# A decoder trunk on one NeuronCore: DeltaNet decays from two shared operands, conv taps and gathers on GpSimd, solve steps placed behind the weight splits

## The chip, the cores and the metric

The kernel runs on one core of one Trainium2 chip. A core has a matrix engine (PE; PEld is its weight loading, which overlaps), a vector engine (DVE), a scalar engine (ACT), a general engine (GpSimd, POOL in the profile) and a queue processor (SP) that issues the DMAs. The engines run side by side; each takes its own instructions strictly in their order, and an instruction waits at the head of its engine until the semaphores it names have been reached. The metric is device time of one execution in microseconds (us), lower is better. "Before" is the median of 3 runs, and the profile is of a further execution.

## The reference

Two layers over 512 positions of 1024 channels. Layer 0 mixes tokens with a gated DeltaNet, layer 1 with a Conformer convolution; each is followed by cross-attention into a memory of 256 rows and a squared-ReLU MLP. Only the DeltaNet is touched. Cut to what matters (8 heads of width 128; chunks of 64 in the reference, of 128 in the kernel):

```python
proj = h @ w_in                                    # q, k, v, z and 16 gate columns
qkv  = silu(causal_depthwise_conv(qkv, w_conv))    # width 4
beta = sigmoid(b_raw)
g    = -exp(a_log) * softplus(a_raw + dt_bias)     # log decay per token and head
g_cum = cumsum(g, axis=-1)                         # inside a chunk
diff  = g_cum[..., :, None] - g_cum[..., None, :]
decay = exp(where(causal, diff, -inf))
lower = where(strict, (k_beta @ k.T) * decay, 0)
sol   = triangular_solve(I + lower, [v*beta, k_beta*exp(g_cum)])
attn_intra = (q @ k.T) * decay
# then the scan over chunks: v_new, o, state
```

## The kernel before

**The stream of units.** All large products run as units. A unit is 24 matmuls of 128x128 weights by 512 columns that fill one PSUM bank: 8 input tiles, each as three products of split numbers (`mm3`: high by high, high by low, low by high). The weights of a unit (128x1024) come by DMA as `raw`; ACT rounds them to `wh` (`wsplit`, L204) and DVE computes the rest `wl` = raw - wh (L205, printed as L72, the line of the helper `tt`). Three such pairs exist (NW = 3), so the pair of a unit can be made only when the unit three places earlier has left PE.

**The DeltaNet stage** covers about the first 330 us. Its units run in the order k0 to k7, v0 to v3, q0 to q3, z (heads 0 to 3), v4 to v7, q4 to q7, z, and then the keys and values of the first cross-attention. Each unit is cut into two halves ("mains"); `run` goes through the mains by number, and after main i it records the side jobs that `S.at(i, rank, ...)` hung there, by rank. k2 is mains 6 and 7, v0 18 and 19, q0 26 and 27, q3 32 and 33, z begins at 34. A scheduler then fixes each engine's order of instructions once, at build time; nothing is reordered on the chip.

**The side jobs of one k head**, which the change touches:

- `gates` (after main 5): from the 16 gate columns `ab` come `beta` and `g`, by about 25 small DVE operations on 128x32 tiles and three ACT exponentials.
- `decay_in`: for each head GpSimd builds `gi` = tri_le times g (128x512), ACT and DVE split it into `gih` and `gil`. `decay`: PE multiplies both with `tri_gt_r` into PSUM, ACT takes the exponential (`dt`), GpSimd multiplies by the mask `tri_le` (L406).
- `conv_head`: DVE scales the unit's PSUM result into `cv`, ACT makes tap 0 (`cva`), and each further tap is either one DVE operation (L422) or an ACT product `cvq` (L419) and a GpSimd addition (L420); CONV_K, CONV_Q and CONV_V say how many taps go the second way. Then ACT applies SiLU.
- `k2`: PE transposes k (`kt`, L440) and forms its Gram matrix (`G`, L444); ACT squares and copies, DVE multiplies with the decay into `bt`, GpSimd scales `bt`.
- `fs_in` (L485): four ACT copies of 32x128 gather the diagonal 32x32 blocks of `bt` into `DB`, for all heads together.

**The solve.** `fs_begin` transposes DB into `FT` on DVE (L499), and `fs_steps` runs 31 steps of two dependent DVE operations each (`fst`, `X`, L508 and L510), with FS = (23, 9): from main 23 on, over 9 mains. `fs_end` transposes twice (`TB`, `UB`). `mg_a` copies the blocks back (ACT to `x0`, GpSimd to `u0`), and `mg_w` and `mg_y` merge them on PE (`mg`, L545 and L557) from main 32 on (MG). `q2` forms `ai` = k times q (L466), `rec` is the scan over the chunks from main 41 on (REC), and both need what stands above.

Of the kernel before, what the change touches and what calls it, by code (L numbers as in the profile page):

```python
# [8 lines left out]
F32 = mybir.dt.float32  # L9
F32R = mybir.dt.float32r  # L10
# [30 lines left out]
def tile_trunk(ctx, tc, xT, memT, prm_d, adt_d, bdw_d, w_ab, w_kq, w_v, w_z, w_dno, w_pw1, w_pw2,  # L41
# [5 lines left out]
    wp = ctx.enter_context(tc.tile_pool(name="wp", bufs=2))  # L47
    fsp = ctx.enter_context(tc.tile_pool(name="fsp", bufs=3))
    up = ctx.enter_context(tc.tile_pool(name="up", bufs=NSLOT))
    sp = ctx.enter_context(tc.tile_pool(name="sp", bufs=16))  # L50
    psp = ctx.enter_context(tc.tile_pool(name="psp", bufs=8, space=bass.MemoryType.PSUM))

    cnt = [0]
# [15 lines left out]
        return cp.tile(list(shape), dt, tag=s, name=s)  # L69

    def tt(e, o, a, b, op):
        e.tensor_tensor(out=o, in0=a, in1=b, op=op)  # L72

    def stt(o, a, s, b, op0, op1):
        dve.scalar_tensor_tensor(out=o, in0=a, scalar=s, in1=b, op0=op0, op1=op1)  # L75
# [43 lines left out]
    for i in range(WARM):  # L119
# [4 lines left out]
    tri_gt = const([P, P], "tri_gt")  # L124
    pool.affine_select(out=tri_gt, in_=ones, pattern=[[-1, P]], compare_op=ALU.is_gt, fill=0.0,
                       base=0, channel_multiplier=1)
    tri_gt_r = const([P, P], "tri_gt_r", F32R)
    act.copy(tri_gt_r, tri_gt)
    ident4 = const([P, 32], "ident4")
    eps_rms = const([P, 1], "eps_rms")  # L130
    pool.memset(eps_rms, EPS)
# [64 lines left out]
    def wsplit():  # L196
        u = ws["split"]
        ws["split"] += 1
        while ws["load"] <= u:
            wload()  # L200
        raw = ws["raw"].pop(u)
        h = wp.tile([P, 1024], F32R, tag="wh", name=nm("wh"), bufs=NW)
        lo = wp.tile([P, 1024], F32R, tag="wl", name=nm("wl"), bufs=NW)
        act.copy(h, raw)  # L204
        tt(dve, lo, raw, h.bitcast(F32), ALU.subtract)  # L205
        ws["hl"][u] = (h, lo)

    def wnext(key, hf):
# [118 lines left out]
    class DeltaNet:  # L327
        def __init__(self, norm):
            self.n, self.xs = norm, norm.xs
            for n, s in ((64, "abt"), (32, "beta"), (32, "g"), (96, "egd"), (32, "sek"), (32, "nk"),  # L330
                         (32, "s_all"), (32, "sdec"), (32, "s_neg"), (32, "sdec_neg"), (32, "ssq"), (4, "tok")):
                setattr(self, s, keepc(n, s))
            for s in ("GI", "DtM", "KT", "Kt", "Ai", "QT", "BT", "U", "VT", "VB", "Z", "OG", "ps", "M"):
                setattr(self, s, {})
            self.DB = self.fs = None
            self.S = [None, None]
# [46 lines left out]
            ts(dve, e2, e1, 1.0, ALU.add)  # L383
            dve.reciprocal(beta, e2)

        def decay_in(self, hs):
            for h in hs:
                gi = slot(s="gi")
                tt(pool, c4(gi), over_c(tri_le), over_i(self.g[:, h * 4:h * 4 + 4]), ALU.mult)
                self.GI[h] = split(gi, "gi")  # L390

        def decay(self, hs):
            if 0 in hs:
                ps_g = psum("gsum")
                pe.matmul(ps_g[:, 0:32], ones, self.g, start=True, stop=True)
                pe.matmul(ps_g[:, 32:64], tri_gt, self.g, start=True, stop=True)
                pe.matmul(ps_g[:, 64:96], tri_le, self.g, start=True, stop=True)
                act.activation(self.egd, ps_g[:, 0:96], AF.Exp)
            for h in hs:
                gh, gl = self.GI.pop(h)  # L400
                ps = psum("dt")
                pe.matmul(ps, tri_gt_r, gh, start=True, stop=False)
                pe.matmul(ps, tri_gt_r, gl, start=False, stop=True)
                dt = slot(s="dt")
                act.activation(dt, ps, AF.Exp)
                tt(pool, c4(dt), c4(dt), over_c(tri_le), ALU.mult)  # L406
                self.DtM[h] = dt

        def conv_head(self, ps, ti, npool, a=None):
# [19 lines left out]
            self.KT[h] = self.conv_head(self.ps.pop(("k", h)), 8 + h, CONV_K)  # L429

        def ev_q(self, h):
            self.M["q", h] = self.conv_head(self.ps.pop(("q", h)), h, CONV_Q)

        def k2(self, h):
            hc = slice(h * 4, h * 4 + 4)
            gq = h // 4
            kT = self.KT[h]
            ps = psum("kt")
            for c in range(4):
                pe.transpose(ps[:, c * P:(c + 1) * P], kT[:, c * P:(c + 1) * P], ident)  # L440
            psg = psum("G")
            for c in range(4):
                cs = slice(c * P, (c + 1) * P)
                pe.matmul(psg[:, cs], kT[:, cs], kT[:, cs], start=True, stop=True)  # L444
            sqk = slot(s="sqk")
            act.activation(sqk, ps, AF.Square)
            kt = slot(s="kt")
            act.copy(kt, ps)
            self.Kt[h] = kt
            bt0 = self.BT[h] = slot(s="bt")  # L450
            tt(dve, bt0, psg, self.DtM[h], ALU.mult)
            ssk = small(4)
            dve.tensor_reduce(out=ssk, in_=c4(sqk), op=ALU.add, axis=AX.X)
            ts(dve, self.sek[:, hc], ssk, EPS, ALU.add)
            rk = small(4)
            dve.reciprocal(rk, self.sek[:, hc])
            tt(dve, self.s_all[:, hc], rk, self.beta[:, hc], ALU.mult)
            tt(pool, c4(bt0), c4(bt0), over_i(self.s_all[:, hc]), ALU.mult)
# [26 lines left out]
        def fs_in(self, h):  # L485
            bt, n = c4(self.BT[h]), h * 4
            if self.DB is None:
                self.DB = fsp.tile([P, 1024], F32, tag="fs", name=nm("DB"))
            db = self.DB.rearrange("p (i n) -> p i n", n=32)
            for b in range(4):  # L490
                bs = slice(32 * b, 32 * b + 32)
                act.copy(db[bs, :, n:n + 4], bt[bs, :, bs].rearrange("p c i -> p i c"))

        def fs_begin(self):
            X = fsp.tile([P, 1024], F32, tag="fs", name=nm("X"))
# [659 lines left out]
    for gq in range(2):  # L1155
        S.at(at["z", "g", gq] + 7, 4, D.ev_z, gq)
    S.at(T_STAT + 3, 0, D.gates)
    S.at(T_STAT + 5, 5, D.decay_in, [0, 1, 2, 3])
    S.at(T_DEC, 2, D.decay, [0, 1])
    S.at(T_DEC + 1, 2, D.decay, [2, 3])  # L1160
    for i, hh in enumerate(([4, 5], [6, 7])):
        S.at(DEC1[i], 5, D.decay_in, hh)
        S.at(DEC1[i] + 2, 2, D.decay, hh)
    for h in range(8):
        S.at(K2[h], 2, D.k2, h)
        S.at(K2[h] + 2, 5, D.fs_in, h)
# [1 line left out]
        S.at(Q2[h] + 1, 3, D.q3, h)  # L1168
    f0, nf = FS
    S.at(f0, 5, D.fs_begin)  # L1170
    for i in range(nf):
        S.at(f0 + i, 6, D.fs_steps, i * 31 // nf, (i + 1) * 31 // nf)
    S.at(f0 + nf, 0, D.fs_end)
    for h in range(8):
        S.at(MGP[h], 5, D.mg_pre, h)
        S.at(MG[h], 1, D.mg_a, h)
        for j, f in enumerate((D.mg_w, D.mg_y, D.mg_y, D.mg_end)):
            S.at(MG[h] + MGLAG + j, 1, f, h)
    for gq in range(2):
        S.at(f0 + 1 + gq, 7, D.norm_k, gq)  # L1180
        for c in range(4):
            S.at(at["v", 4 * gq + 3] + V2[gq], 3, D.v2, gq, c)
        n = 0
        for c in range(4):
            for step in range(3):
                S.at(REC[gq] + n, 0, D.rec, gq, c, step)
                n += 1
            S.at(REC[gq] + n, 5, D.o_gate, gq, c)
        S.at(REC[gq] + n + 1, 1, D.o_norm, gq)
# [117 lines left out]
WARM = 13  # L1307
SQ0 = 8
T_STAT = 2
T_DEC = 10  # L1310
NW = 3
CONV_K, CONV_Q, CONV_V = 0, 1, 3
DEC1 = (11, 13)
K2 = (13, 12, 14, 15, 16, 17, 19, 20)
Q2 = (30, 31, 33, 35, 54, 56, 58, 60)
FS = (23, 9)
MGP = (31, 31, 34, 34, 37, 37, 40, 40)
MG = (32, 32, 35, 35, 38, 38, 41, 41)
MGLAG = 1
V2 = (8, 7)  # L1320
MGAIN = 4
HO = 73
REC = (41, 66)
MEM = 53
MLP_ORDER = [("up", 0), ("up", 1), ("dn", 0), ("up", 2), ("dn", 1), ("up", 3), ("dn", 2), ("dn", 3)]
TAP_RATE = 0.75
# [95 lines left out]
```

## Time and profile before

| | |
|---|---|
| median of 3 runs | 1596.11 us (1595.97 to 1596.54) |
| the profiled execution: its time, its span | 1595.83 us, 1594.1 us |
| mean granted PE clock | 0.985 |
| PE, DVE, ACT, POOL busy | 97%, 56%, 42%, 17% of the span |
| PE busy in the stretches 0-40, 40-80, 80-120, 120-160, 160-200 us | 36.01, 34.26, 36.26, 22.83, 37.30 us |
| PE busy from 200 to 240 and from 400 to 480 us | 40.00 and 80.00 us, that is all of it |

The page gives the busy time of each engine, then strips of 40 slices in tenths. The granted clock is the share of full speed that PE was given: at 1.00 the matmuls of a unit follow each other every 0.23 us, at half clock every 0.43 us. In the timeline, a row has its start in us, its length, engine, line, operation, the tile written, the tiles read, shapes and a count; in brackets the idle time of that engine ahead of it and who ended that. Rows of groups have the busy time and then the mean of one in ns.

### The profile page before, as it was taken

To read this page: it belongs to the slowest core of one execution; us is meant where nothing else is said; L and a number is where in the kernel's file an instruction comes from. 1 tells how busy PE (TensorE), PEld (TensorE's weight loads), DVE (VectorE), ACT (ScalarE), POOL (GpSimd) and SP (SyncE) were. 2 spreads that over 40 slices of the span, in tenths; PEclk is the share of its full clock that TensorE was granted. 3 is DMA by queue.
4 is the path that set the end of the run, shared out by engine and by line. 5 is a ranking of instruction groups with operands and counts; after the bars stand their busy time and mean duration, and the time that the engine had idled before them with its cause. 6 is when DMAs were issued, how large, how long until landed. Compare 5 with 4: busy or idle time off the path is not lost.

```text
span 1594.1 us, 19919 instructions
## 1 busy us (share of the span) xinstructions
PE 1543.3 (97%) x7864; PEld 1304.3 (82%) x7864; DVE 893.1 (56%) x1239; ACT 663.3 (42%) x1014; POOL 273.4 (17%) x310
## 2 busy tenths in 40 slices
PE   8895999999999999999999999899999999999997
PEld 6674888898888888888888889888888888888897
DVE  6969447576455444343445599974445443444443
ACT  6694546545344443241324321264434442323332
POOL 0653434302111100000021316102112000000002
PEclk9997999999999999999999999999999999999999
DMA  5112012254221232322322422252213223222321
GB/s 179 49 58 66 29 65 80 67 186 131 93 66 65 87 101 93 105 94 93 102 96 93 144 81 78 76 171 94 79 40 106 93 93 96 102 93 95 104 93 54
DMA packets 47615, 147.09 MB, mean 92 GB/s; under 512 B 6305, under 2 KB 11041, under 8 KB 47521
## 3 DMA queue, kind: packets, MB, share of 16 engines
q1 hardware_dynamic: 47520, 145.81, 27.6%
q8 instruction: 62, 1.02, 0.3%
q14 instruction: 33, 0.26, 0.0%
HBM read 142.38 MB, written 2.10 MB: 91 GB/s over the span
## 4 chain that ended last, share of the span: by engine, by line
PE 82%; DVE 11%; ACT 3%; issue 2%; POOL 1%; DMA 0%; DVEq 0%; SPq 0%; POOLq 0%; ACTq 0%
PE dn L220 7%; PE dn L222 7%; PE dn L221 7%; PE up L220 7%; PE up L222 7%; PE up L221 7%; DVE ca L75 4%; PE q L220 2%; PE xo L221 2%; PE q L222 2%; PE q L221 2%; PE xo L222 2%; PE xo L220 2%; DVE wl L72 2%; PE pw L220 2%
## 5 line engine op out<-in xcount | busy, mean ns | idle before, releaser
L204 ACT CAST wh<-raw 128x1024 fp32r<-128x1024 f32 x248 | 259.9, 1051 | 690.7 <-PE dn L221 191.5
L72 DVE TENSOR_TENSOR wl<-raw,wh 128x1024 fp32r<-128x1024 f32 x248 | 314.2, 1269 | 130.3 <-ACT wh L204 124.3
L220 PE MATMUL up<-xh,wh 128*128 128x512 f32 x512 | 200.2, 391 | 0.0
L222 PE MATMUL up<-xh,wl 128*128 128x512 f32 x512 | 199.2, 389 | 0.0
L221 PE MATMUL up<-xl,wh 128*128 128x512 f32 x512 | 199.2, 389 | 0.0
L220 PE MATMUL dn<-uh,wh 128*128 128x512 f32 x448 | 174.3, 389 | 0.0
L221 PE MATMUL dn<-ul,wh 128*128 128x512 f32 x448 | 174.3, 389 | 0.0
L222 PE MATMUL dn<-uh,wl 128*128 128x512 f32 x448 | 174.3, 389 | 0.0
L72 DVE TENSOR_TENSOR h<-dn,h 128x512 f32<-128x512 f32 x56 | 41.8, 747 | 170.4 <-PE dn L222 170.4
L75 DVE SCALAR_TENSOR_TENSOR rl<-up,rb 128x512 f32<-128x512 f32 x64 | 44.2, 690 | 157.0 <-PE up L222 157.0
L72 POOL TENSOR_TENSOR tap<-ident,prm 128x512 f32<-128x512 f32 x45 | 60.5, 1373 | 331.4 <-PE up L222 263.8
L221 PEld LDWEIGHTS up<-xl,wh 128*128 128x128 f32 x512 | 96.1, 188 | 20.3 <-issue 0.5
L220 PEld LDWEIGHTS up<-xh,wh 128*128 128x128 f32 x512 | 96.1, 188 | 20.3 <-issue 0.5
L222 PEld LDWEIGHTS up<-xh,wl 128*128 128x128 f32 x512 | 96.1, 188 | 20.1
L222 PEld LDWEIGHTS dn<-uh,wl 128*128 128x128 f32 x448 | 84.1, 188 | 17.5
L221 PEld LDWEIGHTS dn<-ul,wh 128*128 128x128 f32 x448 | 84.1, 188 | 17.4
L220 PEld LDWEIGHTS dn<-uh,wh 128*128 128x128 f32 x448 | 84.1, 188 | 17.4
L72 POOL TENSOR_TENSOR sq<-sq,sq 128x512 f32<-128x512 f32 x30 | 49.7, 1658 | 257.7 <-ACT sq L295 177.0
L220 PE MATMUL h<-xh,wh 128*128 128x512 f32 x192 | 81.2, 423 | 6.1 <-ACT wh L204 3.7
L75 DVE SCALAR_TENSOR_TENSOR ca<-x,prm,ca 128x512 f32<-128x512 f32 x90 | 81.8, 910 | 2.1
L222 PE MATMUL h<-xh,wl 128*128 128x512 f32 x192 | 78.0, 406 | 3.9 <-DVE wl L72 3.9
L221 PE MATMUL h<-xl,wh 128*128 128x512 f32 x192 | 77.8, 405 | 0.3 <-DVE xl L75 0.3
(326 smaller groups left out, 3162.4 us busy)
## 6 DMA issues: line engine op xcount, KB each, us to landing
raw<-w_up SPq DMA_DIRECT2D x64, 512.0 KB, 3.4
raw<-w_dn SPq DMA_DIRECT2D x64, 512.0 KB, 3.4
raw<-w_pw SPq DMA_DIRECT2D x24, 512.0 KB, 3.6
raw<-w_kq SPq DMA_DIRECT2D x16, 512.0 KB, 3.8
raw<-w_k SPq DMA_DIRECT2D x16, 512.0 KB, 3.9
raw<-w_vv SPq DMA_DIRECT2D x16, 512.0 KB, 3.6
raw<-w_q SPq DMA_DIRECT2D x16, 512.0 KB, 3.4
raw<-w_o SPq DMA_DIRECT2D x16, 512.0 KB, 3.6
```

Of the source, the lines that this page charges most:

```text
L72: e.tensor_tensor(out=o, in0=a, in1=b, op=op)
L75: dve.scalar_tensor_tensor(out=o, in0=a, scalar=s, in1=b, op0=op0, op1=op1)
L204: act.copy(h, raw)
L220: pe.matmul(ps, wh, xh, start=first, stop=False)
L221: pe.matmul(ps, wh, xl, start=False, stop=False)
L222: pe.matmul(ps, wl, xh, start=False, stop=last)
```

## The change

- **Decays.** `decay_in` now works for all heads at once. Two operands are made: `R` (128x512) and `L` (128x1024), whose constant halves `decay_const` fills early on GpSimd from two indicator tables `ind` and `headm` (three new DVE reductions beside the setup). When g is there, DVE spreads it to `grep` (128x128), one PE matmul with `tri_mid` makes the sums (`ct`), ACT and DVE split them (`V`), and DVE fills the other halves of R and L. For each head, `decay` adds two products in PSUM: the identity by the mask `later` (0 or -1e30) and a slice of L by R. The exponential of that is `dt`, with no mask after it. The GpSimd `gi`, the splits of `gi` and the GpSimd mask go. `decay_in` hangs at main 5 behind `gates`; the `ct` matmul stands in PE's built order ahead of unit k2.
- **Taps.** CONV_K goes from 0 to 2, CONV_Q from 1 to 3 for heads 0 to 3 (1 stays for 4 to 7).
- **Gathers.** `fs_in` copies with GpSimd in place of ACT.
- **Keys again.** The copy `kt` of heads 4 to 7 moves out of `k2` to `kt2` at mains 60 to 63, which transposes them a second time (16 PE transposes).
- **Solve.** `fs_steps` is recorded under `issue_after(ws["last"])`: in the built order each group of steps stands behind the newest `wl`. FS is (23, 12).
- **Places.** K2, Q2, MGP, MG, REC and the decays move, as the last lines show; the pool of small tiles goes from 16 to 13 buffers.

```diff
     up = ctx.enter_context(tc.tile_pool(name="up", bufs=NSLOT))
-    sp = ctx.enter_context(tc.tile_pool(name="sp", bufs=16))
+    sp = ctx.enter_context(tc.tile_pool(name="sp", bufs=13))
     psp = ctx.enter_context(tc.tile_pool(name="psp", bufs=8, space=bass.MemoryType.PSUM))
...
     def tt(e, o, a, b, op):
-        e.tensor_tensor(out=o, in0=a, in1=b, op=op)
+        return e.tensor_tensor(out=o, in0=a, in1=b, op=op)
     def stt(o, a, s, b, op0, op1):
...
                        base=0, channel_multiplier=1)
-    tri_gt_r = const([P, P], "tri_gt_r", F32R)
-    act.copy(tri_gt_r, tri_gt)
+    ident_r = const([P, P], "ident_r", F32R)
+    act.copy(ident_r, ident)
+    later = const([P, P], "later", F32R)
+    ts(pool, later, tri_le, 1.0, ALU.subtract, 1e30, ALU.mult)
+    tri_mid = const([P, P], "tri_mid")
+    ts(pool, tri_mid, tri_le, tri_le[:, 63:64], ALU.subtract)
+    ind = const([P, 4], "ind")
+    dve.tensor_reduce(out=ind, in_=ident.rearrange("p (x c) -> p c x", c=4), op=ALU.add, axis=AX.X)
+    headm = const([P, 8], "headm")
+    headx = const([P, 32], "headx")
+    dve.tensor_reduce(out=headx, in_=ident.rearrange("p (x c) -> p x c", c=4), op=ALU.add, axis=AX.X)
+    dve.tensor_reduce(out=headm, in_=headx.rearrange("p (a h) -> p h a", h=8), op=ALU.add, axis=AX.X)
     ident4 = const([P, 32], "ident4")
...
         act.copy(h, raw)
-        tt(dve, lo, raw, h.bitcast(F32), ALU.subtract)
+        ws["last"] = tt(dve, lo, raw, h.bitcast(F32), ALU.subtract).ins
         ws["hl"][u] = (h, lo)
...
             for n, s in ((64, "abt"), (32, "beta"), (32, "g"), (96, "egd"), (32, "sek"), (32, "nk"),
-                         (32, "s_all"), (32, "sdec"), (32, "s_neg"), (32, "sdec_neg"), (32, "ssq"), (4, "tok")):
+                         (32, "s_all"), (P, "grep"), (32, "sdec"), (32, "s_neg"), (32, "sdec_neg"), (32, "ssq"), (4, "tok")):
                 setattr(self, s, keepc(n, s))
...
             dve.reciprocal(beta, e2)
-        def decay_in(self, hs):
-            for h in hs:
-                gi = slot(s="gi")
-                tt(pool, c4(gi), over_c(tri_le), over_i(self.g[:, h * 4:h * 4 + 4]), ALU.mult)
-                self.GI[h] = split(gi, "gi")
+        def decay_const(self):
+            self.R = slot(F32R, "R")
+            self.L = fsp.tile([P, 1024], F32R, tag="fs", name=nm("L"))
+            pool.tensor_copy(c4(self.R)[64:128], over_i(ind)[64:128])
+            pool.tensor_copy(self.L.rearrange("p (h j) -> p h j", h=8)[0:64], over_i(headm)[0:64])
+        def decay_in(self):
+            dve.tensor_copy(self.grep.rearrange("p (a x) -> p a x", a=4), over_c(self.g))
+            ps = psum("ct")
+            pe.matmul(ps[:, 0:P], self.grep, tri_mid, start=True, stop=True)
+            v = slot(F32R, "V")[:, 0:P]
+            act.copy(v, ps[:, 0:P])
+            for a in (1, 3):
+                rs = slice(32 * a, 32 * a + 32)
+                tt(dve, v[rs], ps[rs, 0:P], v[rs].bitcast(F32), ALU.subtract)
+            vf = v.bitcast(F32)
+            tt(dve, c4(self.R)[0:64], over_c(vf)[0:64], over_i(ind)[0:64], ALU.mult)
+            stt(self.L.rearrange("p (h j) -> p h j", h=8)[64:128], over_c(vf, 8)[64:128], -1.0,
+                over_i(headm)[64:128], ALU.mult, ALU.mult)
         def decay(self, hs):
...
             for h in hs:
-                gh, gl = self.GI.pop(h)
                 ps = psum("dt")
-                pe.matmul(ps, tri_gt_r, gh, start=True, stop=False)
-                pe.matmul(ps, tri_gt_r, gl, start=False, stop=True)
+                pe.matmul(c4(ps), ident_r, over_c(later), start=True, stop=False)
+                pe.matmul(ps, self.L[:, h * P:(h + 1) * P], self.R, start=False, stop=True)
                 dt = slot(s="dt")
                 act.activation(dt, ps, AF.Exp)
-                tt(pool, c4(dt), c4(dt), over_c(tri_le), ALU.mult)
                 self.DtM[h] = dt
...
         def ev_q(self, h):
-            self.M["q", h] = self.conv_head(self.ps.pop(("q", h)), h, CONV_Q)
+            self.M["q", h] = self.conv_head(self.ps.pop(("q", h)), h, CONV_Q[h // 4])
+        def tr_k(self, h):
+            ps = psum("kt")
+            for c in range(4):
+                pe.transpose(ps[:, c * P:(c + 1) * P], self.KT[h][:, c * P:(c + 1) * P], ident)
+            return ps
+        def kt2(self, h):
+            ps = self.tr_k(h)
+            self.Kt[h] = slot(s="kt")
+            act.copy(self.Kt[h], ps)
         def k2(self, h):
...
             kT = self.KT[h]
-            ps = psum("kt")
-            for c in range(4):
-                pe.transpose(ps[:, c * P:(c + 1) * P], kT[:, c * P:(c + 1) * P], ident)
+            ps = self.tr_k(h)
             psg = psum("G")
...
             act.activation(sqk, ps, AF.Square)
-            kt = slot(s="kt")
-            act.copy(kt, ps)
-            self.Kt[h] = kt
+            if h < 4:
+                self.Kt[h] = slot(s="kt")
+                act.copy(self.Kt[h], ps)
             bt0 = self.BT[h] = slot(s="bt")
...
                 bs = slice(32 * b, 32 * b + 32)
-                act.copy(db[bs, :, n:n + 4], bt[bs, :, bs].rearrange("p c i -> p i c"))
+                pool.tensor_copy(db[bs, :, n:n + 4], bt[bs, :, bs].rearrange("p c i -> p i c"))
         def fs_begin(self):
...
     S.at(T_STAT + 3, 0, D.gates)
-    S.at(T_STAT + 5, 5, D.decay_in, [0, 1, 2, 3])
-    S.at(T_DEC, 2, D.decay, [0, 1])
-    S.at(T_DEC + 1, 2, D.decay, [2, 3])
-    for i, hh in enumerate(([4, 5], [6, 7])):
-        S.at(DEC1[i], 5, D.decay_in, hh)
-        S.at(DEC1[i] + 2, 2, D.decay, hh)
+    S.at(0, 4, D.decay_const)
+    S.at(T_STAT + 3, 1, D.decay_in)
+    for i in range(4):
+        S.at(T_DEC + i, 2, D.decay, [2 * i, 2 * i + 1])
     for h in range(8):
...
     S.at(f0, 5, D.fs_begin)
+    def fs_steps(j0, j1):
+        with tc.issue_after(ws["last"]):
+            D.fs_steps(j0, j1)
     for i in range(nf):
-        S.at(f0 + i, 6, D.fs_steps, i * 31 // nf, (i + 1) * 31 // nf)
+        S.at(f0 + i, 6, fs_steps, i * 31 // nf, (i + 1) * 31 // nf)
     S.at(f0 + nf, 0, D.fs_end)
...
             S.at(MG[h] + MGLAG + j, 1, f, h)
+    for h in range(4, 8):
+        S.at(KT2 + h, 2, D.kt2, h)
     for gq in range(2):
...
 T_STAT = 2
-T_DEC = 10
+T_DEC = 9
 NW = 3
-CONV_K, CONV_Q, CONV_V = 0, 1, 3
-DEC1 = (11, 13)
-K2 = (13, 12, 14, 15, 16, 17, 19, 20)
-Q2 = (30, 31, 33, 35, 54, 56, 58, 60)
-FS = (23, 9)
-MGP = (31, 31, 34, 34, 37, 37, 40, 40)
-MG = (32, 32, 35, 35, 38, 38, 41, 41)
+CONV_K, CONV_Q, CONV_V = 2, (3, 1), 3
+K2 = (11, 12, 13, 14, 15, 16, 18, 20)
+Q2 = (33, 35, 37, 39, 54, 56, 58, 60)
+FS = (23, 12)
+MGP = (35, 35, 37, 37, 40, 40, 42, 42)
+MG = (36, 36, 38, 38, 41, 41, 43, 43)
 MGLAG = 1
...
 HO = 73
-REC = (41, 66)
+REC = (43, 66)
+KT2 = 56
 MEM = 53
```

## The prediction

> **What bounds the kernel now.** I read the page's strips first, then who kept PE waiting, then the clock by stretches, then the timeline of each engine from 28 to 200 us.
>
> ```profile
> span 1594.1 us, 19919 instructions
> ...
> PE   8895999999999999999999999899999999999997
> ...
> PEclk9997999999999999999999999999999999999999
> ```
>
> PE is busy in nearly every slice; the hole is the fourth (120 to 160 us), with a lower clock there. Only what makes PE wait, or adds to its work, can count. The table of PE's waits has the causes, with total us, times and longest:
>
> ```profile
> PE ai L466 <- ACT cva L426: 12.1, 2, 8.6
> PE h L222 <- DVE wl L72: 3.9, 2, 2.4
> ...
> PE h L220 <- ACT wh L204: 3.7, 2, 2.6
> PE dt L403 <- DVE gil L72: 3.5, 4, 1.6
> PE mg L545 <- issue: 2.7, 2, 2.1
> ...
> PE dt L402 <- ACT gih L257: 2.2, 2, 1.1
> ...
> PE kt L440 <- ACT cva L426: 1.3, 1, 1.3
> ```
>
> They sum to 29.4 us, all in the DeltaNet stage: 5.7 for the split decays, 7.6 for weight halves that are not ready, 12.1 where `ai` waits for the SiLU of q0 and q1 whose taps stand in DVE's queue among the solve steps, 2.7 at the first merges. And a long wait costs twice. By stretches (busy of PE, PEld, DVE, ACT, POOL, then granted clock, DMA):
>
> ```profile
> 132.00:136.00 4.00, 4.00 (x10) 3.13 (x11) 3.79 (x7) 2.17 (x3) 1.32 (x1) 0.50 0.69 226
> ...
> 154.00:158.00 4.00, 4.00 (x18) 3.71 (x18) 3.90 (x11) 1.31 (x3) 2.19 (x3) 0.50 0.00 0
> ...
> 162.00:166.00 4.00, 4.00 (x30) 3.70 (x30) 3.12 (x10) 0.00 (x0) 0.00 (x0) 1.00 0.00 0
> ```
>
> After the 8.6 us wait, from 153.1 to 161.4, PE ran at half clock. Read in this way, half clock took 4.1 us there, 2.8 from 131.8 on and about 2.7 around 62 to 69, some 9.6 us up to the first merge at 169.3. So before that merge 29.4 - 0.6 + 9.6 = 38.4 us lie open, and the first merge could not come earlier than about 131.
>
> **The change, part by part. First, a new wait.** The `ct` matmul needs `grep`, so all of `gates`, and stands in PE's built order ahead of k2; 24 matmuls of k2 and all units are queued behind it. Now nothing on PE needs g before 44 us:
>
> ```profile
> 28.29 0.69 DVE L72 TENSOR_TENSOR cv<-h,rb 128x512 f32<-128x512 f32 x1 [1.76 <-ACT rb L318]
> ...
> 29.06 0.72 ACT L415 ACTIVATE cva<-cv,prm 128x512 f32<-128x512 f32 x1 [0.81 <-DVE cv L72]
> ...
> 30.31 0.42 PE L345 MATMUL abT<-ident,ab 16*128 16x16 f32 x4
> ...
> 32.01 1.28 ACT L426 ACT_TABLE_LOAD   x1
> ...
> 37.08 0.17 DVE L79 TENSOR_SCALAR sm<-sm 128x32 f32<-128x32 f32 x1
> ...
> 41.41 0.18 DVE L72 TENSOR_TENSOR g<-sm,sm 128x32 f32<-128x32 f32 x1
> ...
> 99.84 1.94 ACT L419 ACTIVATE cvq<-cv,prm 128x512 f32<-128x512 f32 x3
> ```
>
> PE has done k1 and the gate transposes at 30.31 + 0.42. In the built order DVE's tap of k0 now stands ahead of the gates and waits for two GpSimd additions. All times come 0.6 us later than in the rows, since three small reductions of ident go ahead of DVE's first `xl`, for which PE waits (0.2 each, near the smallest DVE row here, 0.17; by the 512 wide row, 0.69, it would be 2). From 29.7, three ACT products of 0.61 end at 31.5; the additions start when the second is there, 30.9, and take 2 x 1.3: 33.5; DVE's tap (0.65) and ACT's SiLU (0.6) by the rows of the same width, a table load of 1.28 and the exponentials 0.3: 36.4. DVE's chain from there to g took 4.3 us, of it 1.3 two taps that are gone; with g, beta and grep of 0.2, 0.3 and 0.3: 40.2. PE waits from 31.3 to 40.3: **9.0 us**, and like the 8.6 us above this brings half clock, 4.0 us. What it gives: the waits for split decays, 5.7 us, go, as L and R (below 0.7 and 1.2 us on DVE by the widths of `cv` and `wl`) are ready during k2 and k3, 11 us of cover.
>
> **PE's own work.** Decays stay at two matmuls of 512 columns a head. The 16 second transposes are new:
>
> ```profile
> 30.65 0.50 PE L220 MATMUL h<-xh,wh 128*128 128x512 f32 x1
> ...
> 44.20 0.40 PE L222 MATMUL h<-xh,wl 128*128 128x512 f32 x1
> ...
> 71.37 0.60 PE L440 MATMUL kt<-ident,cva 128*128 128x128 f32 x4
> 71.80 1.06 PE L444 MATMUL G<-cva 128*128 128x128 f32 x8
> ```
>
> 60 matmuls of units start between 30.65 and 44.20: 0.23 each. Four transposes take 0.43, so 16 take **1.7 us**, on the path, as PE is full there (z and v units); ct takes 0.2.
>
> **GpSimd's queue in the k units.** Removed are gi and the mask, 24 us; moved in are 16 additions and 32 gathers:
>
> ```profile
> L72 POOL TENSOR_TENSOR cva<-cva,cvq 128x512 f32<-128x512 f32 x16 | 21.3, 1330 | 17.0 <-ACT cvq L419 16.5
> L72 POOL TENSOR_TENSOR gi<-tri_le,g 128x512 f32<-128x512 f32 x8 | 12.5, 1573 | 5.4 <-DVE g L72 5.4
> L72 POOL TENSOR_TENSOR dt<-dt,tri_le 128x512 f32<-128x512 f32 x8 | 11.4, 1453 | 4.8 <-ACT dt L405 4.8
> L537 POOL COPY u<-UB 32x128 f32<-32x128 f32 x24 | 10.8, 452 | 10.9 <-DVE UB L517 9.8
> L72 POOL TENSOR_TENSOR bt<-bt,s_all 128x512 f32<-128x512 f32 x8 | 9.6, 1200 | 6.8 <-DVE s_all L72 6.6
> L527 POOL MEMSET bt<- 32x128 f32 x32 | 6.3, 198 | 8.7 <-ACT DB L492 8.0
> ```
>
> ```profile
> L492 ACT COPY DB<-bt 32x128 f32<-32x128 f32 x32 | 13.3, 416 | 0.6
> ```
>
> A gather on GpSimd is not in the trace: ACT's price (0.42) is the lower end, the dearest eight of the `u` copies (0.54) the upper; I take 0.45, the row of the same shape: 14.4 us, off ACT and onto GpSimd. PE runs k2 from 40.3, 5.5 and 4.0 at half clock, 49.8; k3, 55.3; then six decay pairs, the gate sums, k4 and the first transposes and Gram matrix, 65.4; ACT copies that head and starts k4's taps at 67.8; GpSimd has the first of them at 69.0. From there to the last gather it has 11 additions (14.6), 8 scalings (8.8), 32 gathers (14.4), 28 clears (5.6) and 1.5 of other clears: 44.9 us, and 1.6 of waiting for the second head. It is full: the gathers end at **115.5**, where ACT had them at 116.4 (the FT row below). So relieving ACT starts the solve no earlier. What DVE has queued behind FT is `cv` of v1 and `wl` of q0, needed at 120: covered.
>
> **The solve on DVE**, from FT to TB:
>
> ```profile
> 116.47 1.25 DVE L499 STREAM_TRANSPOSE FT<-DB 128x1024 f32<-128x1024 f32 x1 [0.65 <-ACT DB L492]
> ...
> 118.89 4.03 POOL L72 TENSOR_TENSOR cva<-cva,cvq 128x512 f32<-128x512 f32 x3 [2.19 <-ACT cvq L419]
> 118.98 1.27 DVE L72 TENSOR_TENSOR X<-X,fst 128x31 f32<-128x31 f32 x1
> ...
> 123.32 0.25 DVE L72 TENSOR_TENSOR X<-X,fst 128x87 f32<-128x87 f32 x1
> ...
> 140.02 0.42 DVE L72 TENSOR_TENSOR X<-X,fst 128x252 f32<-128x252 f32 x1
> ...
> 165.30 2.06 DVE L516 STREAM_TRANSPOSE TB<-X 128x1024 f32<-128x1024 f32 x1
> ...
> 169.28 1.10 PE L545 MATMUL mg<-x,bt 128*128 128x96 f32 x8 [2.10 <-issue]
> ```
>
> ```profile
> L72 DVE TENSOR_TENSOR wl<-raw,wh 128x1024 fp32r<-128x1024 f32 x5 | 6.0, 1210 | 0.0
> ...
> L72 DVE TENSOR_TENSOR cv<-h,rb 128x512 f32<-128x512 f32 x4 | 2.7, 681 | 0.0
> ```
>
> Undisturbed, a solve operation repeats every 0.37 us on the mean (0.25 at 87 elements, 0.42 at 252, and a gap of 0.04); 62 take 23.0. With FT and TB (2.4), 8 `wl` at 1.15 (9.2) and 13 operations of 128x512 (7 `cv`, 4 `vb`, 2 `dt`) at 0.6, as rows overlap by some 0.07 (7.8), that is 42.4. The tie has a price: the group behind q1's `wl` waits for its `wh`, which stands in ACT's queue behind v1's SiLU and v2's taps, 3.5 us. And GpSimd's additions hold DVE up: between 118.89 and 122.92 three additions let three small solve operations through, each 1.3 us long. In all nine additions cost 7.7 us there, 0.85 each. Now 21 additions (v1 to q3) fall in this stage, 18 beside DVE work; some meet operations that read PSUM, which are not held, so I take 0.75: 13.5. Sum 59.4: TB ends at 174.9, and after four ACT copies of 0.42 the first merge comes at **176.6**, 7.3 later than the 169.3 above. But in the new order 68 z matmuls, 15.6 us, stand ahead of it, which before came after.
>
> The Trainium skill, page "SBUF — State Buffer", section "SBUF: two separate sides", says that the port pair shared by VectorE and GpSimd is an exclusive lock for the whole instruction, that a VectorE operation with two SBUF inputs against a GpSimd one that reads SBUF falls under it, and that the loser fully blocks. The held solve operations above agree, and taken strictly it speaks against this change: it is the second rival below, 1602.5 us.
>
> **The sum.** First merge +7.3, less 15.6; then ACT has 12 block copies, two w copies, a square and a y copy, 7.2 us, ahead of what the second `mg_y` reads, where PE has 4.6 us of work: PE waits 2.6 us and has some 2 at half clock, where it had 0.6 and 1.5: +2.5; transposes +1.7: **-4.1 us**. The profiled execution took 1595.83 (its span and 1.7 around it): 1591.7; the median of the runs is 0.3 above it: **1592**. The later stages that move (REC by two mains, MG) I put at nothing: PE is busy throughout the sixth slice of the strip above and almost all later ones, their cover is the units between; without it each merge step would show its ACT copy, 0.4 us.
>
> **Rivals.** *The solve ends before PE comes.* PE's own pace: 131 + 0.6 + 9.0 + 4.0 + 0.2 + 15.6, and 7 for SiLUs of k6 and k7 behind GpSimd's queue: 167.4. If additions cost DVE 0.3 each, TB is there, and the sum is -1.9 - 15.6 + 1.0 + 1.7 = -14.8: 1581. For it: most solve operations are larger than those of the row; against it: nine cost 7.7. *DVE is held fully (slower).* If every one of the 18 additions holds DVE for its whole 1.33 us, 24.0 in place of 13.5, the merge comes 10.5 later: +6.4, 1602.5. It decides from about 1.0 us an addition on; the first three rows speak for it, the average against. Gathers at 0.54 would add 2.9. *The change does not do what the order says*: the gates come early and PE does not wait. Then 9 us less ahead of k4, and GpSimd's queue starts as much earlier: -13, 1583. Against it: ct reads grep.
>
> **How the numbers follow.** Chances: the forecast 0.42 (its own range 1586 to 1598), the early solve 0.22, the held DVE 0.30, no gate wait 0.06. 0.2% is 3.2 us, about what a measurement tells from no change; of the forecast 0.23 lies beyond it on the fast side, 0.16 within, 0.03 on the slow side. Faster 0.51, same 0.16, slower 0.33. The range, 1577 to 1606, leaves out a fifth: below, an early solve with gathers at ACT's price; above, a held DVE with dear gathers.
>
> **What would show it.** Right: a wait of `ct` on DVE of 8 to 10 us near 31, no waits of `dt`, GpSimd nearly full from 69 to 115, FT at 113 to 118, TB at 171 to 179 and PE idle ahead of the first merge. Wrong: FT before 110 or after 120; a first merge that finds TB done; PE waits beyond 200 us that were not there before.

## The result, and the profile after

| | before | after |
|---|---|---|
| median of 4 runs each | 1596.04 us (1595.08 to 1596.54) | 1603.72 us (1603.63 to 1606.78) |
| profiled span, mean clock | 1594.1 us, 0.985 | 1602.1 us, 0.985 |
| FT starts, FT to the end of TB, first merge | 116.47, 50.9, 169.28 us | 121.56, 66.8, 189.90 us |
| PE busy 0-40, 40-80, 80-120, 120-160, 160-200 us | 36.01, 34.26, 36.26, 22.83, 37.30 | 27.05, 40.00, 31.64, 33.22, 30.09 |

The change makes the kernel slower by half a per cent: the ratio after to before is 1.0054 (95% interval 1.0036 to 1.0071), some 8 us more where 4 us less were forecast. The page of after shows the hole of the fourth slice spread over the first five:

```profile
span 1602.1 us, 19957 instructions
...
PE   6978799999999999999999999999999999999997
```

Who kept PE waiting (engine, line, released by; total us, times, longest):

```profile
PE ct L409 <- DVE grep L407: 9.4, 1, 9.4
PE kt L463 <- ACT cva L452: 8.4, 3, 6.1
PE z L262 <- DVE wl L72: 7.2, 2, 5.2
...
PE h L230 <- ACT wh L214: 3.2, 1, 3.2
PE z L261 <- DVE cv L72: 3.2, 1, 3.2
PE ai L501 <- ACT bt L582: 2.1, 1, 2.1
...
PE mg L580 <- ACT x L571: 1.1, 1, 1.1
```

The waits for split decays (5.7 us) and the long ones of `ai` (12.1) are gone, as the change means them to be. In their place stand the gates (9.4), `kt` for the SiLUs of later k heads, whose additions stand in GpSimd's queue (8.4), and the z units, whose `wl` and `cv` stand in DVE's queue among the solve steps (10.4). Two places then decide the first merge. First the timeline, GpSimd's part up to FT and what follows:

```profile
67.94 1.28 POOL L72 TENSOR_TENSOR cva<-cva,cvq 128x512 f32<-128x512 f32 x1 [5.17 <-ACT cvq L445]
...
114.53 4.08 POOL L72 TENSOR_TENSOR cva<-cva,cvq 128x512 f32<-128x512 f32 x3
...
119.72 1.80 POOL L527 COPY DB<-bt 32x128 f32<-32x128 f32 x4
...
121.56 1.25 DVE L534 STREAM_TRANSPOSE FT<-DB 128x1024 f32<-128x1024 f32 x1 [5.46 <-POOL DB L527]
...
186.34 2.06 DVE L551 STREAM_TRANSPOSE TB<-X 128x1024 f32<-128x1024 f32 x1
...
189.90 1.10 PE L580 MATMUL mg<-x,bt 128*128 128x96 f32 x8 [1.09 <-ACT x L571]
```

Before, FT waited 0.65 us for ACT; now DVE stands idle 5.46 us until GpSimd has copied the last block. Then a close look at the solve, GpSimd's row first and DVE's below it:

```profile
138.71 4.03 POOL L72 TENSOR_TENSOR cva<-cva,cvq 128x512 f32<-128x512 f32 x3 [2.87 <-ACT cvq L445]
...
138.57 0.27 DVE L72 TENSOR_TENSOR fst<-FT,X 128x112 f32<-128x112 f32 x1
138.87 1.25 DVE L72 TENSOR_TENSOR X<-X,fst 128x112 f32<-128x112 f32 x1
140.15 1.36 DVE L72 TENSOR_TENSOR fst<-FT,X 128x135 f32<-128x135 f32 x1
141.55 1.34 DVE L72 TENSOR_TENSOR X<-X,fst 128x135 f32<-128x135 f32 x1
142.92 0.32 DVE L72 TENSOR_TENSOR fst<-FT,X 128x156 f32<-128x156 f32 x1
```

Three additions on GpSimd, and DVE completes one solve operation for each (DVE is "held"): 1.25 to 1.36 us where the operations just outside take 0.27 and 0.32.

### The profile page after: what moved, and what is told of

It reads as the page before. It is cut to its first block, busy times and chain, and to the rows that moved or that the text cites. A ratio compares the mean times of both kernels' runs of the same rounds, so it can differ in the third digit from the quotient of the medians.

```text
span 1602.1 us, 19957 instructions
## 1 busy us (share of the span) xinstructions
PE 1545.5 (96%) x7882; PEld 1307.0 (82%) x7882; DVE 884.2 (55%) x1215; ACT 658.0 (41%) x997; POOL 305.3 (19%) x354
## 3 DMA queue, kind: packets, MB, share of 16 engines
q8 instruction: 62, 1.02, 0.3%
## 4 chain that ended last, share of the span: by engine, by line
PE 81%; DVE 11%; POOL 4%; issue 2%; ACT 2%; DMA 0%; DVEq 0%; SPq 0%; POOLq 0%; ACTq 0%
PE dn L230 7%; PE dn L232 7%; PE dn L231 7%; PE up L230 7%; PE up L231 7%; PE up L232 7%; DVE ca L75 4%; DVE wl L72 2%; PE q L230 2%; PE xo L231 2%; PE q L231 2%; PE xo L232 2%; PE q L232 2%; PE xo L230 2%; POOL cva L72 2%
```

## The experiments

All times are device us of one core; each ratio is to the kernel before, run on the same chip beside it, whose median was 1595.4 to 1595.6 (1596.0 beside after). In the table "solve" is from the start of FT to the end of TB, read from each kernel's timeline. "After" is the changed kernel.

| run | time | ratio (95%) | FT | solve | first merge |
|---|---|---|---|---|---|
| after | 1603.7 | 1.0054 (1.0036 to 1.0071) | 121.56 | 66.8 | 189.90 |
| after, ct at main 8 | 1603.0 | 1.0045 (1.0033 to 1.0058) | 118.86 | 66.9 | 187.22 |
| after, 21 additions left out | 1584.2 | 0.9929 (0.9915 to 0.9942) | 121.33 | 45.4 | 168.19 |
| after, gathers on ACT | 1599.9 | 1.0023 (1.0014 to 1.0032) | 119.66 | 59.1 | 180.27 |
| after, no tie | 1602.9 | 1.0047 (1.0033 to 1.0061) | 121.41 | 64.2 | 187.12 |
| after, k taps on DVE | 1593.9 | 0.9986 (0.9977 to 0.9995) | 110.07 | 68.1 | 179.72 |
| after, one q tap on GpSimd | 1598.4 | 1.0017 (1.0009 to 1.0026) | 122.58 | 62.5 | 186.60 |
| after, all taps on DVE, gathers on ACT | 1572.3 | 0.9854 (0.9840 to 0.9867) | 106.73 | 51.0 | 159.16 |
| the same, ct at main 8 | 1568.3 | 0.9830 (0.9816 to 0.9843) | 103.41 | 51.0 | 155.83 |
| the same, gathers on GpSimd, ct at main 5 | 1575.2 | 0.9871 (0.9857 to 0.9884) | 106.32 | 53.3 | 161.02 |
| all taps on DVE, gathers on ACT, no tie | 1572.9 | 0.9857 (0.9844 to 0.9871) | 107.93 | 51.0 | 160.38 |
| before, with the new decays | 1598.1 | 1.0012 (1.0003 to 1.0021) | 116.36 | 54.1 | 172.33 |
| before, all taps on DVE | 1587.3 | 0.9946 (0.9933 to 0.9960) | 111.51 | 49.1 | 162.91 |

**The gates later.**

```diff
-    S.at(T_STAT + 3, 1, D.decay_in)
+    S.at(T_STAT + 6, 1, D.decay_in)
...
-T_DEC = 9
+T_DEC = 10
```

> The ct product and the operands L and R hang at main 8 in place of main 5, the decays at mains 10 to 13 in place of 9 to 12; all else as in the changed kernel (1603.7 us). Theory (a serial chain: the gates wait of 9.4 us and the half clock behind it delay k4, so GpSimd's stream from 67.94 on, so the solve, so the first merge at 189.90): PE goes on into k2 at about 30.5, the wait for grep falls to under 2 us, GpSimd's first addition of k4 comes at 56 to 60, the first merge at 177 to 181, and the time is 1590 to 1595 us. Rival (the wait is cover: GpSimd and DVE fill the room, PE waits as long at kt or ahead of the first merge): the first merge at 186 or later, 1599 us or more.

The rival's numbers held. PE went on into k2, but the wait only shrank (PE's waits first, then rows of the timeline):

```profile
PE ct L409 <- DVE grep L407: 4.6, 1, 4.6
```

```profile
37.60 2.67 POOL L72 TENSOR_TENSOR cva<-cva,cvq 128x512 f32<-128x512 f32 x2 [2.96 <-ACT cvq L445]
...
38.99 1.33 DVE L79 TENSOR_SCALAR sm<-sm 128x32 f32<-128x32 f32 x1
...
42.79 2.67 POOL L72 TENSOR_TENSOR cva<-cva,cvq 128x512 f32<-128x512 f32 x2 [1.20 <-ACT cvq L445]
...
42.58 2.92 DVE L75 SCALAR_TENSOR_TENSOR sm<-sm,sm 128x32 f32<-128x32 f32 x4
...
118.86 1.25 DVE L534 STREAM_TRANSPOSE FT<-DB 128x1024 f32<-128x1024 f32 x1 [5.18 <-POOL DB L527]
```

The chain that ends in `g` now meets the additions of k1 and k2: four operations of 128x32, 0.19 each elsewhere, took 2.92 us, with two additions on GpSimd from 42.79 on. The `TENSOR_SCALAR` at 38.99 has only one input and was held as well, 1.33 us where 0.17 is usual. GpSimd's first addition of k4 came 4.8 us earlier (63.12), FT and the first merge 2.7, so a little over half of the shorter wait came through. The time fell by 0.7 us, less than can be told from nothing (the intervals of the two ratios overlap almost wholly).

**The additions left out.** The sums of the GpSimd taps of v1 to v3 and q0 to q3 are not made.

```diff
-                    tt(pool, a, a, b, ALU.add)
+                    if ti not in (0, 1, 2, 3, 17, 18, 19):
+                        tt(pool, a, a, b, ALU.add)
```

> Leaves out the 21 GpSimd additions of the taps of v1 to v3 and q0 to q3 (the ACT products are made, their sums are not), so v and q of these heads are other numbers. All else as in the changed kernel. Theory (18 additions hold DVE about 1.2 us each, not 0.75): from FT to the end of TB it takes 43 to 48 us in place of 66.8, and no solve operation longer than 0.6 us is left; FT comes about 4 us earlier, as three of the additions (4.08 us) stand ahead of the scaling of k7. Rival (the solve is long because steps and wl wait for wh, the tie): it still takes 56 us or more; by the price of 0.75 an addition it would take 53. The time is then set by where PE itself arrives, 170 to 176: 1587 to 1592 us by the theory, 1595 or more by the rival.

The theory held in the solve, but FT did not move: the three additions at 114.53 are those of v0, which this run keeps. The time, 1584.2 us, is 3 us below the theory's band. The solve fell by 21.5 us (66.84 - 45.37), 1.02 for each of the 21 additions. Most of this is longer DVE operations. By stretches, first of after, then without the additions (busy of PE, PEld, DVE, ACT, POOL, each with its number of operations, then granted clock, DMA):

```profile
121.50:188.45 66.95, 52.15 (x223) 41.17 (x221) 60.09 (x87) 33.08 (x50) 35.33 (x40) 0.87 0.19 63
```

```profile
121.30:166.75 45.45, 42.70 (x209) 34.66 (x207) 40.05 (x87) 31.53 (x49) 4.74 (x18) 1.00 0.27 93
```

The same 87 DVE operations took 60.09 us and 40.05: 20.0 of hold, 0.95 an addition. The other 1.4 us are idle time, of it 1.0 of waiting for `wh`. The groups inside the solve show who is held (count | busy us, mean ns | idle before and who ended it), first of after, then without the additions:

```profile
L72 DVE TENSOR_TENSOR wl<-raw,wh 128x1024 fp32r<-128x1024 f32 x8 | 13.3, 1668 | 4.8 <-ACT wh L214 4.8
L72 DVE TENSOR_TENSOR cv<-h,rb 128x512 f32<-128x512 f32 x7 | 4.7, 677 | 0.0
...
L72 POOL TENSOR_TENSOR cva<-cva,cvq 128x512 f32<-128x512 f32 x21 | 30.9, 1470 | 23.1 <-ACT cvq L445 22.0
```

```profile
L72 DVE TENSOR_TENSOR wl<-raw,wh 128x1024 fp32r<-128x1024 f32 x8 | 9.7, 1218 | 3.8 <-ACT wh L214 3.8
L72 DVE TENSOR_TENSOR cv<-h,rb 128x512 f32<-128x512 f32 x7 | 4.7, 678 | 0.0
```

`wl`, which reads two tiles of SBUF, takes 1.67 us beside the additions and 1.22 without; `cv`, which reads PSUM, takes 0.68 in both. The wait for `wh` is there in both (4.8 and 3.8) and not the cause. The Trainium skill, page "SBUF — State Buffer", section "SBUF: two separate sides", excepts neither long nor short operations from the lock that it states and names two conditions on DVE's side, a 2-port performance mode or two SBUF inputs; the pair of `wl` and `cv` agrees with the second. The one-input operation at 38.99 above would need the first; in which mode it ran, no trace here shows.

**Gathers on ACT.**

```diff
-                pool.tensor_copy(db[bs, :, n:n + 4], bt[bs, :, bs].rearrange("p c i -> p i c"))
+                act.copy(db[bs, :, n:n + 4], bt[bs, :, bs].rearrange("p c i -> p i c"))
```

> The 32 gathers of DB go back to ACT, all else as in the changed kernel. Theory (GpSimd is the bound of the k stage, the gathers cost it 16.9 us from 71 to 121.5 and DVE's chain behind it): FT comes at 113 to 117 in place of 121.56, the first merge 4 to 7 us earlier, 1597 to 1600 us. Rival (ACT takes the place as the bound, since its SiLUs and tap products then stand behind 13 us of gathers): FT at 119 or later, the time within 2 us of 1603.7 or above.

The time falls in the theory's band, the path is the rival's: FT came only 1.9 us earlier. GpSimd had done the last scaling at 114.4, but on ACT a `wh` and the tap products of a v head stood ahead of the last four gathers:

```profile
113.39 1.04 POOL L72 TENSOR_TENSOR bt<-bt,s_all 128x512 f32<-128x512 f32 x1
...
117.90 1.74 ACT L527 COPY DB<-bt 32x128 f32<-32x128 f32 x4
```

The other 7.7 us were won inside the solve. The wait for `wh` is 1.1 us there in place of 4.8, and two additions, a `wl` and a `cv` less fall in it (19, 7 and 6); no `wl` meets an addition any more (mean 1.22), but solve operations do instead. So the first merge came 9.6 us earlier, but the time fell by 3.8 only (5.7 between the two profiled executions). One part of this is order: 12 fewer z matmuls stand ahead of the first merge than in after (56 and 68 records in the two traces), and at 0.23 each these 2.8 us come behind it. Ahead of the merge PE has a wait that was not there:

```profile
PE ssq L515 <- DVE vb L72: 4.2, 1, 4.2
```

**No tie.** `fs_steps` is recorded without `issue_after`.

> The groups of solve steps are recorded without the tie to the newest wl, all else as in the changed kernel. Theory (the tie is a minor term: one wait of 4.0 us for the wh of one unit): from FT to TB it takes 62 to 67 us in place of 66.8, the time is 1600 to 1606 us. Rival (the tie makes the solve long, steps stand behind weights that are late): 58 us or less, 1597 us or less.

The theory held: 0.8 us, nothing that can be told. The solve was 2.6 us shorter, PE's waits in z 7.4 in place of 10.4, and the merges waited 0.9 longer for `x`. DVE still waits 3.2 us for `wh` in the solve (4.8 with the tie), so most of the wait that the prediction put down to the tie is not the tie's.

**The k taps on DVE.** CONV_K = 0.

> CONV_K is 0 again: the 16 GpSimd additions and 16 ACT products of the k taps become 16 DVE taps; all else as in the changed kernel (1603.7 us). Theory (GpSimd's queue bounds the k stage, and the SiLUs of k6 and k7 wait in it, so PE's 8.4 us at kt): kt waits fall under 2 us, FT comes at 108 to 114 in place of 121.56, the time is 1592 to 1598 us. Rival (gathers and scalings alone keep GpSimd the bound, or DVE's 10 us more of taps do): FT at 118 or later, 1600 us or more.

The theory held: `kt` waits are gone from the list, FT comes 11.5 us earlier, the time falls by 9.8. FT still waits for GpSimd's gathers, and DVE is idle for longer before it:

```profile
110.07 1.25 DVE L534 STREAM_TRANSPOSE FT<-DB 128x1024 f32<-128x1024 f32 x1 [8.93 <-POOL DB L527]
```

The solve took 68.1 us, no less than in after: the additions of v and q go with it.

**One q tap on GpSimd.** CONV_Q = (1, 1).

> CONV_Q is (1, 1): 8 of the 21 GpSimd additions of the solve stage, two taps of each of q0 to q3, become DVE taps of about 0.65 us; all else as in the changed kernel. Without all 21 additions the stretch from FT to the end of TB was 46.7 - 1.3 = 45.4 us in place of 66.8, 1.02 an addition. Theory (held DVE): 8 x (1.02 - 0.65) = 3.0 us less, FT to TB 62 to 65 us, the time 1599 to 1602 us. Rival (the taps come late among the solve steps, so PE waits at ai as it did before the change): ai waits of 5 us or more, 1603 us or more.

The theory's direction held and its size was short: the solve fell by 4.3 us (62.5), the time by 5.3. `ai` waits for no SiLU. Eight additions out and eight taps in saved 4.3. If each addition that left was worth 1.02, a tap cost DVE about 1.02 - 4.3 / 8 = 0.48 us, an estimate, and less than its row (0.75).

**All taps on DVE, gathers on ACT.** CONV = 0, (0, 0), 0 and the edit of the gathers.

> All conv taps of k, v and q on DVE (CONV 0, (0, 0), 0) and the gathers on ACT: GpSimd has no additions and no gathers left; decays, tie and places as in the changed kernel. Theory (GpSimd's queue and its hold on DVE are the whole loss): FT at 107 to 113, from FT to TB 45.4 and some 21 taps of 0.65, 59 us, TB done at 166 to 173, the time 1584 to 1592 us, below the kernel before. Rival (DVE, with 24 us of taps more, becomes the bound itself): TB done at 178 or later, 1595 us or more.

The theory's direction held, and every number went past its band: 1572.3 us, 31.4 below after and 23 below before. The timeline has FT 14.8 us earlier, and the group of taps inside the solve shows 20 of them, none of them held:

```profile
106.73 1.25 DVE L534 STREAM_TRANSPOSE FT<-DB 128x1024 f32<-128x1024 f32 x1 [0.39 <-ACT DB L527]
...
155.65 2.07 DVE L551 STREAM_TRANSPOSE TB<-X 128x1024 f32<-128x1024 f32 x1
...
159.16 1.10 PE L580 MATMUL mg<-x,bt 128*128 128x96 f32 x8 [1.37 <-issue]
```

```profile
L75 DVE SCALAR_TENSOR_TENSOR cva<-cv,prm,cva 128x512 f32<-128x512 f32 x20 | 14.9, 744 | 0.0
```

With 14.9 us more work of its own, DVE does the solve in 51.0 us in place of 66.8. The 45.4 us of the run without additions hold 3.8 of waiting for `wh`, and 1.9 for one `wl` and one `cv` that here come before FT; against the 39.7 that remain, 20 taps added 11.3 us, 0.57 each. One reason is in the rows: DVE operations that do not need each other overlap (in after, `X` at 143.28 takes 0.32 us, and `cv` begins 0.24 after it). By stretches as above, after and then this run:

```profile
80.00:120.00 40.00, 31.64 (x151) 26.14 (x149) 20.00 (x37) 17.32 (x27) 34.24 (x68) 0.91 0.13 48
120.00:160.00 40.00, 33.22 (x143) 26.24 (x141) 32.74 (x40) 23.68 (x36) 23.63 (x28) 0.91 0.20 66
```

```profile
80.00:120.00 40.00, 38.04 (x187) 31.66 (x186) 34.77 (x69) 30.25 (x53) 10.10 (x31) 1.00 0.23 80
120.00:160.00 40.00, 36.87 (x190) 30.79 (x188) 39.21 (x81) 14.40 (x23) 4.66 (x13) 1.00 0.18 66
```

From 120 to 160 us DVE is nearly full, and yet earlier done; PE has 10 us more busy time in these 80 and the full clock.

**The same, with the gates later** (the edit of the first experiment).

> The kernel with all taps on DVE and the gathers on ACT (1572.3 us, PE's wait at ct 8.0) with ct, L and R at main 8 and the decays at mains 10 to 13. In the changed kernel the same move took 4.8 us off the wait, 2.7 off the start of the solve and 0.7 off the time. Theory (GpSimd's queue was the cover; without it the chain from PE through ACT and DVE to FT runs as early as k is there): FT moves 3 us or more ahead of 106.73, the time is 1563 to 1569 us. Rival (the k stage has other slack, or PE's wait comes back at kt): FT within 2 us, 1571 to 1574 us.

The theory's bands held: FT 3.3 us earlier, the first merge 3.3, the time 1568.3. This is the fastest kernel of the study, 1.7% below before.

```profile
PE ct L409 <- DVE grep L407: 2.0, 1, 2.0
```

But its reason, that GpSimd's queue was the cover, is not shown. Of 6.0 us less wait 3.3 reached the first merge, a share of 0.55; behind the full queue it was 2.7 of 4.8, a share of 0.56. The times, 4.0 us here and 0.7 there, look unlike, but the intervals of the ratios allow the same gain in both.

**All taps on DVE, gathers on GpSimd.** CONV = 0, (0, 0), 0 alone.

> All taps on DVE as in the run of 1572.3 us, but the 32 gathers on GpSimd as the change has them. Theory (gathers cost only by making GpSimd's queue full; with no additions it is half empty): FT within 2 us of 106.73, the time 1571 to 1575 us. Rival (the gathers themselves hold DVE, as additions do, some 0.4 us each): FT at 111 or later, DVE operations of 1 us and more beside the gathers, 1577 us or more.

Near the theory: FT at 106.32 is as it said, and 1575.2 us is 0.2 beyond its band, 2.9 above the run with the gathers on ACT. The intervals of the two ratios overlap, so this is at the edge of what can be told. A gather takes longer here than in after, 0.59 us in place of 0.49 (group of GpSimd from 60 to 115 us):

```profile
L527 POOL COPY DB<-bt 32x128 f32<-32x128 f32 x32 | 18.8, 589 | 1.8
```

**All taps on DVE, gathers on ACT, no tie.**

> The run of 1572.3 us without the tie of the solve steps to the newest wl. Theory (the tie is a minor term, as in the changed kernel, where it is 0.8 us): 1570 to 1575 us. Rival (with GpSimd out of the way the tie is what lets each wl come in time for z): PE waits for wl in the z units of 5 us or more, 1577 us or more.

The theory held: 0.7 us apart. The tie does nothing measurable in either setting.

**Before, with the new decays alone.** L, R, ct and the mask in PSUM; CONV, gathers, solve and places of before.

> The kernel before (1595.5 us in these runs) with the new decays alone: L, R, the mask in PSUM and ct behind the gates; taps, gathers, solve and places as before. Theory (the gates wait is mostly cover, as the run with the gates later suggests, where 4.8 us less of it moved the end by 0.7): PE waits 9 to 12 us at ct, the dt waits (5.7 us) are gone, FT at 112 to 117, the time 1592 to 1598 us. Rival (wait and half clock are passed on whole): 1602 to 1608 us.

Neither quite: 1598.1 us, at the edge of the theory's band. FT stands where it stood (116.36; before 116.47), and PE came to the first `ai` 5.7 us earlier than before (134.09 against 139.82), so the 8.1 us at ct were more than made good by the waits that went. But the SiLU of q0 did not come earlier: PE waits 19.1 us at `ai` where before had 12.1, and the solve took 3 us longer:

```profile
PE ai L488 <- ACT cva L448: 19.1, 2, 10.0
PE ct L405 <- DVE grep L403: 8.1, 1, 8.1
```

**Before, all taps on DVE.**

```diff
-CONV_K, CONV_Q, CONV_V = 0, 1, 3
+CONV_K, CONV_Q, CONV_V = 0, 0, 0
```

> The kernel before (1595.4 us) with all taps on DVE: CONV_V from 3 and CONV_Q from 1 to 0, nothing else of the change. Theory (the additions cost the solve 7.7 us before; what the changed kernel without them gains comes mostly from the later q2, merges and recurrence and the lighter decays, which take the waits of 12.1 us at ai away): those waits stay at 8 us or more and the time is 1588 to 1596 us. Rival (the additions were the loss of both kernels, and the other parts of the change give nothing): 1570 to 1580 us.

The theory held in kind, 0.7 us below its band: 1587.3 us, and `ai` still waits:

```profile
PE ai L466 <- ACT cva L426: 15.2, 2, 8.0
```

So the additions cost the kernel before 8 us too, and the rest of the change (decays, places, order, with the gathers on ACT) is worth 1587.3 - 1572.3 = 15.0 us once they are gone. Which part of it gives this, no run isolates; the decays alone, in the kernel before, gave nothing.

## Why the prediction was wrong

It was wrong in the sum of the forecast, at the first merge: 176.6 us foretold, 189.90 measured. Put into its own last line, -4.1 + 13.3 gives +9.2 us; the spans differ by 8.0. Two of its own signs of being wrong came: FT after 120 (121.56), and a new wait of PE beyond 200 us (2.1 for `bt`, up to 202.50). The 13.3 have two parts.

**The price of an addition in the solve (+7.4).** The sum took 0.75 us of held DVE for 18 additions, 13.5; the run without them measured 21.5, 1.02 for each of the 21, or 1.19 for each of the 18. The rest of that sum was right as a whole: 59.4 - 13.5 = 45.9 foretold without additions, 45.4 measured (8.0 - 0.5 is 7.5, against the 7.4 by which the solve exceeds 59.4), though FT and TB were put at 2.4 where their rows, 1.25 and 2.06, sum to 3.3. The step that failed is "some meet operations that read PSUM, which are not held". Such operations were indeed not held (`cv` 0.68), but seven of them are 4.7 us in a stretch in which GpSimd adds for 30.9: a two-input operation soon follows and is held. The average of 0.85 over the nine additions of before, taken for all 21, would have given 17.9 of the 20.0 us of hold; it was the two discounts, from 0.85 to 0.75 and from 21 to 18, that made it 13.5. Nor is the price the whole 1.33 us of the second rival, since the held operation does its own 0.3 to 0.4 us of work within it: 1.33 - 0.35 = 0.98, near the 0.95 measured.

**GpSimd's queue in the k stage (+6.0).** The last gather was to end at 115.5 and ended at 121.52, though the first addition of k4 came at 67.94 and not 69.0. The work between, by groups of after from 67.9 to 121.6:

```profile
L527 POOL COPY DB<-bt 32x128 f32<-32x128 f32 x32 | 15.7, 489 | 1.6
L72 POOL TENSOR_TENSOR cva<-cva,cvq 128x512 f32<-128x512 f32 x11 | 14.2, 1288 | 5.8 <-ACT cvq L445 5.2
L72 POOL TENSOR_TENSOR bt<-bt,s_all 128x512 f32<-128x512 f32 x8 | 10.2, 1277 | 2.5 <-DVE s_all L72 2.4
```

Gathers 15.7 (14.4 foretold), additions 14.2 (14.6), scalings 10.2 (8.8) and 7.3 of clears (7.1): 2.5 us more work. The other 4.6 are idle, 6.2 in place of 1.6: mostly waits for `s_all` and the small gaps ahead of 32 copies and 29 clears. (Of the 5.8 beside the additions, 5.2 lie ahead of 67.94 and do not count.) "It is full" was taken without gaps. The view that GpSimd bounds this stage was right: the k taps on DVE brought FT forward by 11.5 us.

**The gates.** The size of the wait was right (9.0 foretold, 9.4 measured, no `dt` waits after it); the half clock behind it was put too high: from 40.10 to 44.91 eleven gaps between matmuls took 4.81 us, where 0.23 each make 2.5, so 2.3 us against 4.0. And the weight was wrong: the sum passes 13 us of wait and half clock on in full. Of what the later gates took off the wait, 0.56 and 0.55 reached the first merge, so the third rival's -13 was mis-sized too. Where the rest goes was not traced.

**PE's order.** The 15.6 us of z ahead of the first merge were right. By the forecast's own rule, a change of the time equals that of the first merge less 15.6, and 4.2 for later waits and transposes, the run without additions should stand at -12.5 against before and the run with all taps on DVE at -21.5; measured are -11.3 and -23.1. The rule is good to some 3 us: one q tap on GpSimd should stand at +5.9 and stands at +3.0, and the gathers on ACT at -0.4, where +4.4 is measured (+2.3 in the profiled execution). There the 12 z matmuls that come behind the merge, 2.8 us, are part of it; the 4.2 us for `vb` lie ahead of the merge and are not. Of the terms kept out of the sum or put low as minor, the tie was minor (0.8 us), and the three reductions take 0.85 us by their rows, with PE's wait for `xl` 1.3 where it was 0.3. What the later places cost, no run isolates; no new wait stands beyond 205 us.

**The rivals.** The held DVE came true, 1602.5 foretold against 1603.7, by a sum of holds that was too large (24.0 against 20.0) and an FT that was too early, so partly by luck. The early solve is what the kernel does once additions leave GpSimd; it was priced on additions of 0.3 us, which no run shows.

The Trainium skill, page "Perfetto Trace Analysis", section "Optimizing Scalar/DVE Operations", warns that work moved between GpSimd and VectorE might not help, as they share a port; here it did harm, 1.02 us of the solve for an addition against 0.48 to 0.75 for the tap that it replaces.

## What to carry to other kernels

An engine that is relieved by a neighbour is not relieved if the neighbour's work holds it: compare what an operation costs the busy engine itself (0.75 us at most for a tap) with what it costs while the other one does it (1.02), and count the hold for every one of the neighbour's operations, without a discount for those that might miss it. A wait far ahead of what decides is passed on only in part (0.55 and 0.56 in the two places where it was tried); follow such a move through the traces, since times of 0.7 and 4.0 us can look like a law and lie within their intervals. And a change of many parts can hide a good half: here the same edit without its moves to GpSimd beats the kernel before by 1.5%.

## What the runs showed of the hardware that was not expected

Small operations are not spared: some of 128x32, 0.17 to 0.19 us elsewhere, lasted as long as a whole addition (1.33 us for one, and four in 2.92 beside two additions), and one of them has a single input. It seems to work both ways: in after an addition took 1.29 us in the k stage and 1.47 in the solve, where DVE is busier, and a gather 0.49 in after and 0.59 beside DVE's taps; no run isolates this. And a DVE tap among the solve steps cost less than its row of 0.75 us, 0.48 by one estimate and 0.57 by another.
